# A trunk kernel with routed experts: gates applied at a place's last down product, plain turns of the small chunks, and VectorE in program order

## The chip, the cores and the metric

The kernel runs on one core of a Trainium2 chip. The core has TensorE for matrix products (PE in the profile), VectorE (DVE), ScalarE (ACT), GpSimd (POOL) and SyncE (SP), which here issues the loads of the weights; 16 DMA engines move the data. The metric is device time in microseconds (us) of one execution; less is better. All arithmetic is in float32. Where a product needs the precision of float32 at the pace of a rounded form, an operand is split in two rounded halves (a high and a low one) and the product is made of three.

## The reference, cut to what matters

The network has two layers. Each mixes 256 latent and 256 context tokens of width 1024 by three kinds of heads and then runs a feed-forward part. In the first layer that part is dense. In the second it is a choice of 2 among 8 experts per latent token, and only there does the change move work:

```python
def swiglu(h, wg, wu, wd):
    return (jax.nn.silu(h @ wg) * (h @ wu)) @ wd

def moe_ffn(h, w_r, wg, wu, wd):
    logits = (h @ w_r).astype(jnp.float32)
    top_v, top_i = lax.top_k(logits, TOP_K)
    gates = jax.nn.softmax(top_v, axis=-1)
    combine = jnp.sum(jax.nn.one_hot(top_i, N_EXPERTS, dtype=jnp.float32) * gates[..., None], axis=-2).astype(h.dtype)
    out = jnp.zeros_like(h)
    for e in range(N_EXPERTS):
        out = out + combine[..., e:e + 1] * swiglu(h, wg[e], wu[e], wd[e])
    return out
...
x = x + mod[5] * f        # f: what the experts gave; mod[5]: a factor per output column
```

Each expert has a gate and an up matrix of 1024 x 2816 and a down matrix of 2816 x 1024. All are read from HBM once: 264 pieces of 1 MB.

## The kernel before, in words

Tokens are sorted to the experts, and the experts by their load into eight places. Places 1, 0 and 2 are wide (128 slots for tokens), places 3, 4 and 5 have 64 slots, and places 7 and 6 have 32. A ninth set of 32 slots, the rest, holds what place 0 can't take. An expert's hidden width of 2816 is worked off in 11 chunks of 256 columns: two pieces of weights for gate and up, one for down.

A wide place takes each piece split: ScalarE writes the high half (`whi`, line 275), VectorE the low one (`wlo`, line 276), and TensorE multiplies with both into the bank `gu` (gate and up) and then the two banks `py` (down, `down`, line 1701). The small places are multiplied straight from the raw piece (`wraw`). Their chunk comes out with the slots in rows and must be turned: `narrow_mid` (line 1571) copies it to SBUF as `mid`, `turn` (line 1576) turns it on TensorE into the bank `mTx`, and `turned` (line 1584) makes silu times up from it (`silx`), which `down_small` (line 1735) multiplies into the bank `pys`. A 32-slot chunk lies in `mid` as two partial sums, one for each half of the contraction. Before, its turn is a product with a matrix `sel` of 64 columns, which adds the two on the way; a 64-slot chunk is turned by a plain transpose with the identity (`const`). The wide chunk's own product `sil` is transposed into a bank `mT` and split into `mh` and `ml`.

`rounds` (line 1523) interleaves them. First come rounds of place 7 alone; then the 11 rounds of place 1, the 11 of place 0 and the 11 of place 2, each round with one wide chunk and one or two small ones beside it (place 0's rounds have the rest as well); then two rounds of place 6 alone. Place 6 is the last.

When a place has had its last down product, a finish runs (`finishes` and `finish`, lines 1747 and 1754). VectorE multiplies the sum in PSUM with mod[5] into `y`, ScalarE and VectorE split `y` into `yh` and `yl`, TensorE multiplies both with the transposed one-hot `ohT` of the place (a bank `sc`), and VectorE adds the result, times the gate, to the output tile `acc`. A wide place does this in two halves of 512 columns, one after the other. `ohT` is made by `onehot` (line 1492): two compares on VectorE (`oh`), two transposes, a copy on ScalarE. Only one finish is under way at a time, whatever the place.

`sc`, `ohT`, `mT`, `mTx` and `xe` share two banks of PSUM in turn, so that each of them waits until the one before the last has been read.

Order. The program is emitted by a foreground (`experts`) and by background generators that it polls (`finish`, `onehot`, `gather`); a clock kept by estimates decides which step is emitted next and when a piece's split is due. For the experts' part `MSB` says which engines keep that sequence: in `"pa"` TensorE and ScalarE do, and VectorE's instructions are put in order by the scheduler of the tile framework. SyncE loads the weights through seven raw buffers.

Of the kernel before, what the change touches and what calls it, by code (L numbers as in the profile page):

```python
# [18 lines left out]
P = 128  # L19
D = 1024  # L20
KB = D // P
# [4 lines left out]
NE = 8  # L26
# [3 lines left out]
EPS = 1e-6  # L30
# [179 lines left out]
def until(cond):  # L210
    while not cond():
        yield 0.5
# [128 lines left out]
class Net:  # L341
# [1150 lines left out]
    def onehot(self, p):  # L1492

        nc = self.nc
        yield from until(lambda: len(self.ohT) < 2)
        self.ohT[p] = None
        oh = self.mp.tile([P, 2, P], F32, tag="oh1", name="oh1", bufs=1)
        n = self.slots(p)
        for t in range(2):
            nc.vector.tensor_scalar(oh[:, t, :].rearrange("p (a b) -> p a b", b=n), self.c("iota", 0, n).unsqueeze(1).to_broadcast([P, P // n, n]),  # L1500
                                    self.pos0[:, t, 0:1] if p == NE - 1 else self.pos[:, t, p:p + 1], None, op0=ALU.is_equal)
        yield 1.5
        pt = self.bank("ohT")
        for t in range(2):
            self.tp(pt[:, P * t:P * t + P], oh[:, t, :])
        ohT = self.mp.tile([P, 2, P], F32R, tag="ohT", name="ohT", bufs=2)
        nc.scalar.activation(ohT.rearrange("p a b -> p (a b)"), pt[:, :256], AF.Copy)
        yield 1.0
        self.ohT[p] = ohT

    SU = 4.0
    YB, YH = 1, 1
# [63 lines left out]
    def turn(self, pt, at, v, m):  # L1576
        for j in range(2):
            b = v[:, P * j:P * j + P]
            if m == 32:
                self.mm(pt[:, at + 64 * j:at + 64 * j + 64], b, self.sel, True, True)  # L1580
            else:
                self.tp(pt[:, at + P * j:at + P * j + P], b)

    def turned(self, pt, at, m):

        src = pt[:, at:at + 4 * m].rearrange("p (j g s) -> p j g s", j=2, g=2)
        s = self.mp.tile([P, 2, m], F32, tag=f"silx{m}", name="silx", bufs=5 if m == 32 else 4)
        self.act_fn(s, src[:, :, 0, :], AF.Silu)
        self.nc.vector.tensor_tensor(s, s, src[:, :, 1, :], op=ALU.mult)
        return s  # L1590

    def experts(self):
# [4 lines left out]
        nc, o = self.nc, self.o  # L1597
        self.xe, self.ohT, self.py = {}, {}, {}
        self.finishing = False
        self.ndone = 0  # L1600
        self.sel = self.mp.tile([P, 64], F32, name="sel", bufs=1)
        nc.vector.tensor_tensor(self.sel, self.c("ident", 0, 64), self.c("swap", 0, 64), op=ALU.add)
        o.spawn(self.gather(0), 2)
        pw, pn = None, []
        for w, ns in self.rounds() + [(None, [])]:
# [5 lines left out]
            if w:  # L1611
                p, c = w
                x = self.xe[p]
# [3 lines left out]
                for i in range(2):  # L1617
                    t = self.w.get(("gu", p, c, i))
# [34 lines left out]
            mids = []  # L1653
# [23 lines left out]
            if mids:  # L1677
                pt, at = self.bank("mTx"), 0
                for *_, m, v in mids:
                    self.turn(pt, at, v, m)  # L1680
                    at += 4 * m
            pw = None
            if w:
                pm = self.bank("mT")
                for j in range(2):
                    self.tp(pm[:, P * j:P * j + P], sil[:, P * j:P * j + P])
                mh = self.mp.tile([P, 256], F32R, tag="mh", name="mh", bufs=1)
                ml = self.mp.tile([P, 256], F32R, tag="ml", name="ml", bufs=1)
                self.split(mh, ml, pm[:, :256])
                pw = [*w, mh, ml, None]  # L1690
            at = 0
            for p, c, m, v in mids:
                mx = self.turned(pt, at, m)
                at += 4 * m
                if p == NE:
                    pw[4] = mx
                else:
                    pn.append((p, c, mx))
            yield

    def down(self, p, c, mh, ml):
# [12 lines left out]
        if z and p:  # L1714
            self.o.spawn(self.finishes(p), 1)
        return w

    def down_rest(self, w, c, mx):
# [13 lines left out]
        if c == NCH - 1:  # L1732
            self.o.spawn(self.finishes(0), 1)

    def down_small(self, p, c, mx):
# [8 lines left out]
        if c == NCH - 1:  # L1744
            self.o.spawn(self.finishes(p), 1)

    def finishes(self, p):
        yield from until(lambda: not self.finishing)
        self.finishing = True
        for q in (p, NE) if p == 0 else (p,):  # L1750
            yield from self.finish(q)
        self.finishing = False

    def finish(self, p):

        nc = self.nc
        m = self.slots(p)
        parts = P // m
        w = 512 if m > 32 else 256
        yield from until(lambda: self.ohT.get(p) is not None)  # L1760
        ohT = self.ohT[p]
        for n in range(2 if m == P else 1):
            yh, yl = (self.mp.tile([P, 512], F32R, tag=nm, name=nm, bufs=self.YH) for nm in ("yh", "yl"))
# [8 lines left out]
            yield 3.0  # L1772
            for g in (n,) if m == P else range(parts):
                cs = slice(w * g, w * g + w)
                rows = slice(m * g, m * g + m) if parts > 1 else slice(0, P)
                for t in range(2):
                    pz = self.bank("sc")
                    for i, v in enumerate((yh, yl)):
                        self.mm(pz[:, :w], ohT[rows, t, :], v[rows, :w], i == 0, i == 1)
                    nc.vector.scalar_tensor_tensor(self.acc[:, t, cs], pz[:, :w], self.gate[:, t, p:p + 1], self.acc[:, t, cs],  # L1780
                                                   op0=ALU.mult, op1=ALU.add)
                    if self.ndone == NE:
                        nc.sync.dma_start(self.out[P * t:P * t + P, cs], self.acc[:, t, cs])
                    yield 1.0
        del self.ohT[p]
        self.ndone += 1

# [80 lines left out]
    MSA, MSB = "", "pa"  # L1868
# [6 lines left out]
    def run(self):  # L1875
# [7 lines left out]
        with tc.tile_pool(name="keep", bufs=1) as keep, ExitStack() as self.pools, ExitStack() as self.kax, tc.tile_pool(name="sm", bufs=2) as self.sp, \  # L1883
# [3 lines left out]
            self.csil = keep.tile([P, KB, 38], F32, name="csil")  # L1887
            self.eps = keep.tile([P, 1], F32, name="eps")
            self.modT = [keep.tile([P, 48, 2], F32, name=f"modT{l}") for l in range(2)]
            self.wr = keep.tile([P, KB, NE], F32, name="wr")  # L1890
            self.acoef = keep.tile([P, 16], F32, name="acoef")
            self.nsink = keep.tile([P, 16], F32, name="nsink")
            nc.scalar.dma_start(self.csil, d["cT"])
            self.act_fn(self.csil, self.csil, AF.Silu)
            nc.scalar.dma_start(self.params, d["params"])
            nc.scalar.dma_start(self.const[:, :2 * P], d["consts"][:, :2 * P])
            nc.vector.memset(self.eps, EPS)
            self.act_fn(self.acoef, self.par("a_log"), AF.Exp)
            nc.vector.tensor_scalar(self.acoef, self.acoef, -1.0, None, op0=ALU.mult)
            nc.vector.tensor_scalar(self.nsink, self.par("sink"), -1.0, None, op0=ALU.mult)  # L1900
            self.nb, self.nc_banks = 4, 3
            self.w = Weights(self, self.plan(), self.nraw, self.nhi)
            with tc.tile_pool(name="psA", bufs=4, space=PSUM) as self.pp, tc.tile_pool(name="g", bufs=self.ng) as self.gp:
                self.ka = self.kax.enter_context(tc.tile_pool(name="keepA", bufs=1))
                self.gb = self.kax.enter_context(tc.tile_pool(name="act", bufs=2 * KB))
# [39 lines left out]
```

## Time and profile before

| what | us |
| --- | --- |
| three runs | 1587.26, 1581.52, 1585.33 |
| median | 1585.33 |
| the profiled execution | 1583.83 |
| its span, first to last instruction | 1582.1 |

The profile is of one execution on one core. The experts' part takes roughly its last third, from about 900 us on. The profile's page gives the busy time of each engine and the span in 40 slices; the trace answers questions on stretches (the windows) and on single instructions in order of time (the timeline). A timeline row has the start, the duration, the engine, the line, the operation, output and inputs, a count, and in brackets how long the engine had sat idle and which instruction released it. The mean granted clock of TensorE is 0.978 of full speed.

### The profile page before, as it was taken

The page shows a single profiled execution, that of the slowest core. Times are in us where ns is not written, and L with a number is a line of the kernel's source. Part 1 is how long each engine was busy: PE and PEld are TensorE (multiplying, and loading weights), DVE is VectorE, ACT ScalarE, POOL GpSimd, SP SyncE. Part 2 cuts the span into 40 slices and gives each one's busy share as a digit, 9 for nine tenths or more (in the row PEclk, how much of TensorE's full clock was granted, in tenths as well). Part 3 has the DMA queues.
Part 4 walks back from the last instruction along what each step waited for, and adds up shares of the span by engine and source line. Part 5 has one row for each costly group of instructions (what it writes and reads, how often), then busy time and mean ns, then how long its engine had stood idle before and what let it go on. Part 6 is the DMA issues. An engine that isn't in the chain of part 4 may idle for free. (4 is left out here: it accounts for less than half of the span.)

```text
span 1582.1 us, 23498 instructions
## 1 busy us (share of the span) xinstructions
PE 1500.2 (95%) x9302; PEld 1081.1 (68%) x9303; DVE 821.2 (52%) x1481; ACT 666.7 (42%) x1189; POOL 102.6 (6%) x135
## 2 busy tenths in 40 slices
PE   5999998899999999999999899999999999999997
PEld 1766675787887787878757776666566666656654
DVE  2687568543232333378774344544465444654545
ACT  3566644443222312266455354444343443433441
POOL 1200123210000000030300000000000000000000
PEclk9999999999999999999999899999999999999998
DMA  9422055333323323333164499999998999999994
GB/s 372 152 106 107 28 211 202 133 133 112 129 91 149 133 107 113 112 141 142 56 267 181 152 418 419 419 419 420 418 390 358 371 413 417 419 402 407 419 420 158
DMA packets 57715, 396.10 MB, mean 250 GB/s; under 512 B 6528, under 2 KB 8576, under 8 KB 10496
## 3 DMA queue, kind: packets, MB, share of 16 engines
q1 hardware_dynamic: 56016, 392.03, 62.2%
q10 hardware_dynamic: 1584, 2.52, 0.4%
q8 instruction: 75, 1.23, 0.3%
q14 instruction: 40, 0.33, 0.1%
HBM read 393.47 MB, written 1.05 MB: 249 GB/s over the span
## 5 line engine op out<-in xcount | busy, mean ns | idle before, releaser
L276 DVE TENSOR_TENSOR wlo<-wraw,whi 128x1024 fp32r<-128x1024 f32 (+2 forms) x318 | 377.0, 1222 | 161.2 <-ACT whi L275 155.9
L275 ACT ACTIVATE whi<-wraw 128x1024 fp32r<-128x1024 f32 (+2 forms) x318 | 320.0, 1047 | 148.5 <-PE fd L374 57.9
L374 PE MATMUL gu<-whi,xw 128*128 128x512 f32 x528 | 169.1, 401 | 4.2 <-ACT whi L275 4.2
L374 PE MATMUL gu<-wraw,xs 128*64 128x256 f32 (+1 forms) x1760 | 166.2, 386 | 0.5 <-ACT xs L1484 0.5
L374 PEld LDWEIGHTS gu<-wraw,xs 128*64 128x64 f32 (+1 forms) x1760 | 94.4, 127 | 64.3 <-issue 14.6
L374 PEld LDWEIGHTS gu<-whi,xw 128*128 128x128 f32 x528 | 96.9, 190 | 24.5 <-ACT whi L275 6.1
L374 PE MATMUL gu<-wlo,xw 128*128 128x512 f32 x264 | 104.9, 397 | 3.5 <-DVE wlo L276 3.5
L1162 DVE TENSOR_TENSOR fsil<-fsil,fu 128x512 f32<-128x512 f32 x22 | 15.1, 688 | 153.5 <-PE fu L374 118.2
L374 PE MATMUL pys<-wraw,silx 128*32 128x256 f32 (+1 forms) x616 | 87.6, 480 | 6.8 <-DVE y L1770 4.1
L425 ACT ACTIVATE fsil<-fg 128x512 f32<-128x512 f32 x22 | 13.1, 598 | 174.3 <-PE fg L374 174.3
L1573 ACT ACTIVATE mid<-gu 128x256 f32<-128x256 f32 x55 | 21.0, 382 | 137.1 <-PE gu L374 137.1
L374 PE MATMUL fg<-ahi,whi 128*128 128x512 f32 (+1 forms) x192 | 72.3, 377 | 0.0
L374 PE MATMUL fg<-alo,whi 128*128 128x512 f32 (+1 forms) x192 | 71.6, 373 | 0.2 <-POOL alo L523 0.2
L374 PE MATMUL fg<-ahi,wlo 128*128 128x512 f32 (+1 forms) x192 | 71.4, 372 | 0.0
L374 PE MATMUL fu<-alo,whi 128*128 128x512 f32 (+1 forms) x192 | 71.4, 372 | 0.0
L374 PE MATMUL fu<-ahi,wlo 128*128 128x512 f32 (+1 forms) x192 | 71.3, 372 | 0.0
L374 PE MATMUL fu<-ahi,whi 128*128 128x512 f32 (+1 forms) x192 | 71.3, 372 | 0.0
L374 PE MATMUL fd<-mhi,whi 128*128 128x512 f32 (+1 forms) x188 | 70.7, 376 | 0.0
L374 PE MATMUL fd<-mlo,whi 128*128 128x512 f32 (+1 forms) x188 | 70.6, 375 | 0.0
L374 PE MATMUL fd<-mhi,wlo 128*128 128x512 f32 (+1 forms) x188 | 70.6, 375 | 0.0
L374 PE MATMUL modp<-wraw,csil 128*32 128x512 f32 x384 | 56.7, 628 | 12.0 <-ACT csil L425 6.9
L374 PEld LDWEIGHTS gu<-wlo,xw 128*128 128x128 f32 x264 | 49.9, 189 | 18.3 <-DVE wlo L276 7.4
(342 smaller groups left out, 2831.8 us busy)
## 6 DMA issues: line engine op xcount, KB each, us to landing
wraw<-in_moe_dram SPq DMA_DIRECT2D x264, 1024.0 KB, 12.6
wraw<-in_wmod_dram SPq DMA_DIRECT2D x48, 1024.0 KB, 6.4
wraw<-in_fgu_dram SPq DMA_DIRECT2D x22, 1024.0 KB, 4.8
wraw<-in_win_dram SPq DMA_DIRECT2D x16, 1024.0 KB, 4.9
wraw<-in_wout_dram SPq DMA_DIRECT2D x8, 1024.0 KB, 6.2
wraw<-in_fdn_dram SPq DMA_DIRECT2D x8, 1024.0 KB, 6.2
wraw<-in_fdn_dram SPq DMA_DIRECT2D x4, 768.0 KB, 4.9
wraw<-in_wgd_dram SPq DMA_DIRECT2D x2, 1056.0 KB, 4.9
```

Of the source, the lines that this page charges most:

```text
L275: nc.scalar.activation(hi[:, cs], t[:, cs], AF.Copy)
L276: nc.vector.tensor_tensor(lo[:, cs], t[:, cs], hi[:, cs].bitcast(F32), op=ALU.subtract)
L374: self.nc.tensor.matmul(out, l, r, start=start, stop=stop)
L425: self.last_act = self.nc.scalar.activation(out, in_, func, **kw)
L1162: self.nc.vector.tensor_tensor(s, s, pu, op=ALU.mult)
L1573: self.nc.scalar.activation(v, ps[:, :256], AF.Copy)
```

## The change

Five things. (1) The multiplication by mod[5] and the split into halves (`halves`) are emitted at once when a place's last down product is emitted, not when the finish's turn comes; for wide places both halves of the columns, in a buffer `fin`. Wide and narrow finishes no longer wait for each other, only for one of their own kind. The scatter products `sc` follow later. (2) A 32-slot chunk is turned by two plain transposes of 128 columns; ScalarE then copies one partial sum out of the bank to a tile `sum`, and VectorE adds the other, before silu. Two turns share one bank, the wide chunk's among them. (3) VectorE too follows the program's sequence in the experts' part (`MSB = "pad"`). (4) Three `ohT` buffers instead of two. (5) Some small tiles of the first part move to a pool that is freed before the experts' part. The instructions of GpSimd and SyncE stand in the same order before and after, and so does everything ahead of the experts' part on the other engines.

```diff
     def onehot(self, p):
-        yield from until(lambda: len(self.ohT) < 2)
+        yield from until(lambda: len(self.ohT) < 3)
...
-    def turn(self, pt, at, v, m):
+    def turn(self, pt, at, v):
         for j in range(2):
-            b = v[:, P * j:P * j + P]
-            if m == 32:
-                self.mm(pt[:, at + 64 * j:at + 64 * j + 64], b, self.sel, True, True)
-            else:
-                self.tp(pt[:, at + P * j:at + P * j + P], b)
+            self.tp(pt[:, at + P * j:at + P * j + P], v[:, P * j:P * j + P])
 
     def turned(self, pt, at, m):
-        src = pt[:, at:at + 4 * m].rearrange("p (j g s) -> p j g s", j=2, g=2)
+        src = pt[:, at:at + 256]
+        if m == 32:
+            v = src.rearrange("p (j r c) -> p j r c", j=2, r=2)
+            src = self.mp.tile([P, 2, 64], F32, tag="sum32", name="sum32", bufs=2)
+            self.nc.scalar.activation(src, v[:, :, 0, :], AF.Copy)
+            self.nc.vector.tensor_tensor(src, src, v[:, :, 1, :], op=ALU.add)
+            src = src.rearrange("p j (g s) -> p j g s", g=2)
...
-            if mids:
-                pt, at = self.bank("mTx"), 0
-                for *_, m, v in mids:
-                    self.turn(pt, at, v, m)
-                    at += 4 * m
+            jobs = [[x, x[3]] for x in mids] + ([[None, sil]] if w else [])
+            for i, x in enumerate(jobs):
+                if i % 2 == 0:
+                    pt = self.bank("mT" if i + 1 == len(jobs) else "mTx")
+                self.turn(pt, 256 * (i % 2), x[1])
+                x[1] = pt
...
         if z and p:
-            self.o.spawn(self.finishes(p), 1)
+            self.finished(p)
...
+    def halves(self, p):
+        nc, m = self.nc, self.slots(p)
         parts = P // m
         w = 512 if m > 32 else 256
-            yh, yl = (self.mp.tile([P, 512], F32R, tag=nm, name=nm, bufs=self.YH) for nm in ("yh", "yl"))
+        if m == P:
+            f = self.mp.tile([P, 2, KB, P], F32R, tag="xw", name="fin", bufs=2).rearrange("p a k s -> p (a k s)")
+            ys = [(f[:, 1024 * n:1024 * n + 512], f[:, 1024 * n + 512:1024 * n + 1024]) for n in range(2)]
+        else:
+            ys = [tuple(self.mp.tile([P, 512], F32R, tag=nm, name=nm, bufs=1) for nm in ("yh", "yl"))]
+        for n, (yh, yl) in enumerate(ys):
             y = self.mp.tile([P, 512], F32, tag="xsum", name="y", bufs=self.YB)
...
+    def finished(self, p):
+        self.o.wait(lambda: not self.finishing[self.wide(p)])
+        self.o.spawn(self.finishes(p), 1)
+        self.o.poll()
+
+    def finish(self, p, ys):
...
+        yield max(3.0, self.w.splits - self.o.clk + 3.0)
+        yield from until(lambda: self.ohT.get(p) is not None)
+        ohT = self.ohT[p]
+        if p == self.last:
+            yield from until(lambda: self.ndone == NE)
...
-    MSA, MSB = "", "pa"
+    MSA, MSB = "", "pad"
```

Where the rounds of place 1 end and those of place 0 begin, VectorE had this order before. `y<-py` is the gating of place 1, `acc` the additions of its scatter, `wlo` the splits for place 0, `ml` the split of place 0's first chunk, and `y<-pys` the gating of a 64-slot place that ends in the same round.

```order
L1766 TENSOR_TENSOR y<-py,mod5row 128x512
L438 TENSOR_TENSOR yl<-y,yh 128x512
L1766 TENSOR_TENSOR y<-py,mod5row 128x512
L1780 SCALAR_TENSOR_TENSOR acc<-sc,gate,acc 128x512 x2
L276 TENSOR_TENSOR wlo<-wraw,whi 128x1024 x4
L438 TENSOR_TENSOR yl<-y,yh 128x512
L438 TENSOR_TENSOR ml<-mT,mh 128x256
L1589 TENSOR_TENSOR silx<-silx,mTx 128x64
L1770 TENSOR_TENSOR y<-pys,mod5row 64x512
L1589 TENSOR_TENSOR silx<-silx,mTx 128x128
```

In the changed kernel VectorE has this at the same place; `fin` is the low half of the split of `y`.

```order
L438 TENSOR_TENSOR fin<-y,fin 128x512
L276 TENSOR_TENSOR wlo<-wraw,whi 128x1024
L1500 TENSOR_SCALAR oh_9283<-const,pose 128x128 x2
L276 TENSOR_TENSOR wlo<-wraw,whi 128x1024
L1806 SCALAR_TENSOR_TENSOR acc<-sc,gate,acc 128x512
L276 TENSOR_TENSOR wlo<-wraw,whi 128x1024 x2
L1806 SCALAR_TENSOR_TENSOR acc<-sc,gate,acc 128x512 x2
L1767 TENSOR_TENSOR y<-pys,mod5row 64x512 x2
L438 TENSOR_TENSOR yl<-y,yh 128x512
L438 TENSOR_TENSOR ml<-mT,mh 128x256
L1587 TENSOR_TENSOR sum_9359<-sum_9359,mTx 128x128
```

The one-hot compares, three of place 1's additions and the gating of the 64-slot place now stand ahead of `ml`.

On TensorE the same place reads so in the changed kernel, from the last half of the 64-slot chunk to place 0's next wide chunk.

```order
L374 MATMUL sc<-fin,ohT 128x512 x2
L379 MATMUL ohT<-const,oh_9283 128x128 x2
L374 MATMUL gu<-wraw,xs_7662 64x256 x8
L374 MATMUL sc<-fin,ohT 128x512 x2
L374 MATMUL pys<-wraw,silx 64x512 x4
L374 MATMUL sc<-fin,ohT 128x512 x2
L379 MATMUL mTx<-const,mid 128x128 x4
L379 MATMUL mT<-const,sil 128x128 x2
L374 MATMUL sc<-fin,ohT 128x512 x2
L374 MATMUL gu<-whi,xw 128x512 x2
```

Before, two of the four scatter products stood ahead of `mTx`, the other two stood among place 0's products behind it, and the transposes of the one-hot came a round later.

At the end of the program VectorE had this order before, from the gating of place 2 (`y<-py`) to that of the last place (`y<-pys` with 32x256); `silx` with 128x64 is place 6's.

```order
L1780 SCALAR_TENSOR_TENSOR acc<-sc,gate,acc 128x512
L1589 TENSOR_TENSOR silx<-silx,mTx 128x64
L1780 SCALAR_TENSOR_TENSOR acc<-sc,gate,acc 128x512
L438 TENSOR_TENSOR yl<-y,yh 128x512
L1770 TENSOR_TENSOR y<-pys,mod5row 64x512 x2
L1589 TENSOR_TENSOR silx<-silx,mTx 128x64
L1780 SCALAR_TENSOR_TENSOR acc<-sc,gate,acc 128x512 x2
L438 TENSOR_TENSOR yl<-y,yh 128x512
```

In the changed kernel the end of VectorE's order is this.

```order
L1806 SCALAR_TENSOR_TENSOR acc<-sc,gate,acc 128x512
L1767 TENSOR_TENSOR y<-pys,mod5row 64x512 x2
L438 TENSOR_TENSOR yl<-y,yh 128x512
L1587 TENSOR_TENSOR sum_12686<-sum_12686,mT 128x128
L1593 TENSOR_TENSOR silx<-silx,sum_12686 128x64
L1806 SCALAR_TENSOR_TENSOR acc<-sc,gate,acc 128x512 x5
L1500 TENSOR_SCALAR oh_12739<-const,pos 128x128 x2
L1587 TENSOR_TENSOR sum_12745<-sum_12745,mT 128x128
L1593 TENSOR_TENSOR silx<-silx,sum_12745 128x64
L1806 SCALAR_TENSOR_TENSOR acc<-sc,gate,acc 128x512 x2
L1767 TENSOR_TENSOR y<-pys,mod5row 32x256 x4
```

Six additions and the last one-hot now stand ahead of the last chunk's `silx`, where three stood before.

## Rows read from the trace of the kernel before

**Rows 1.** The page: busy time of each engine, its share, its instructions.

```profile
PE 1500.2 (95%) x9302; PEld 1081.1 (68%) x9303; DVE 821.2 (52%) x1481; ACT 666.7 (42%) x1189; POOL 102.6 (6%) x135
```

**Rows 2.** Windows: length, busy us of PE, PEld, DVE, ACT, POOL; clock, DMA, GB/s.

```profile
1000.00:1100.00 100.00, 96.62 (x660) 63.69 (x653) 45.98 (x57) 45.72 (x76) 0.00 (x0) 1.00 1.01 419
1100.00:1200.00 100.00, 95.04 (x667) 60.65 (x669) 54.48 (x82) 38.33 (x64) 0.00 (x0) 0.98 0.96 395
1200.00:1300.00 100.00, 99.62 (x826) 67.73 (x818) 46.37 (x63) 45.41 (x77) 0.00 (x0) 1.00 0.95 385
...
1380.00:1390.00 10.00, 5.88 (x32) 2.13 (x26) 5.86 (x7) 1.75 (x3) 0.00 (x0) 0.77 1.01 419
1400.00:1410.00 10.00, 10.00 (x85) 5.69 (x85) 5.04 (x7) 2.87 (x5) 0.00 (x0) 1.00 0.93 350
1440.00:1450.00 10.00, 10.00 (x64) 6.68 (x64) 4.89 (x7) 4.19 (x7) 0.00 (x0) 1.00 0.98 367
```

**Rows 3.** Timeline of PE where place 1 ends and place 0 begins.

```profile
1142.84 0.66 PE L374 MATMUL mTx<-sel,mid 128*128 128x64 f32 x4
1143.34 0.39 PE L379 MATMUL mTx<-const,mid 128*128 128x128 f32 x2
1143.56 0.38 PE L379 MATMUL mT<-const,sil 128*128 128x128 f32 x2
1143.70 0.71 PE L374 MATMUL gu<-whi,xw 128*128 128x512 f32 x2
...
1147.36 0.50 PE L374 MATMUL sc<-yh,ohT 128*128 128x512 f32 x1 [0.66 <-DVE ml L438]
```

**Rows 4.** Timeline of DVE at the same place.

```profile
1133.04 0.69 DVE L1766 TENSOR_TENSOR y<-py,mod5row 128x512 f32<-128x512 f32 x1 [0.59 <-PE py L374]
...
1141.75 4.62 DVE L276 TENSOR_TENSOR wlo<-wraw,whi 128x1024 fp32r<-128x1024 f32 x4
```

**Rows 5.** Groups by form on DVE and ACT, 1100 to 1582 us: busy, mean ns.

```profile
L276 DVE TENSOR_TENSOR wlo<-wraw,whi 128x1024 fp32r<-128x1024 f32 x138 | 162.8, 1220 | 71.5 <-ACT whi L275 70.9
L1780 DVE SCALAR_TENSOR_TENSOR acc<-sc,gate,acc 128x512 f32<-128x512 f32 x24 | 17.8, 750 | 28.0 <-PE sc L374 27.7
L438 DVE TENSOR_TENSOR ml<-mT,mh 128x256 fp32r<-128x256 f32 x24 | 10.2, 423 | 39.5 <-ACT mh L437 39.0
L1589 DVE TENSOR_TENSOR silx<-silx,mTx 128x128 f32<-128x128 f32 x24 | 6.8, 283 | 5.5 <-ACT silx L425 5.5
L438 DVE TENSOR_TENSOR yl<-y,yh 128x512 fp32r<-128x512 f32 x9 | 6.2, 685 | 1.0 <-ACT yh L437 1.0
L1770 DVE TENSOR_TENSOR y<-pys,mod5row 64x512 f32<-64x512 f32 x6 | 4.1, 687 | 0.1
L425 ACT ACTIVATE silx<-mTx 128x128 f32<-128x128 f32 x24 | 6.6, 276 | 9.8 <-DVE silx L1589 9.8
L437 ACT ACTIVATE yh<-y 128x512 fp32r<-128x512 f32 x9 | 5.6, 625 | 9.1 <-DVE y L1766 5.4 <-PE sc L374 3.7
```

**Rows 6.** Timeline of PE around place 0's first wide products.

```profile
1120.42 0.73 PE L374 MATMUL gu<-whi,xw 128*128 128x512 f32 x2 [2.37 <-ACT whi L275]
...
1122.75 1.05 PE L374 MATMUL gu<-whi,xw 128*128 128x512 f32 x2
...
1126.58 0.62 PE L374 MATMUL gu<-whi,xw 128*128 128x512 f32 x2
```

**Rows 7.** Timeline of PE where place 0 ends and place 2 begins.

```profile
1387.12 3.68 PE L374 MATMUL pys<-wraw,silx 128*64 128x512 f32 x8 [4.12 <-DVE y L1770]
```

**Rows 8.** Timeline of PE at the end.

```profile
1561.05 1.07 PE L374 MATMUL pys<-wraw,silx 128*32 128x256 f32 x16 [0.67 <-DVE silx L1589]
...
1570.88 0.57 PE L374 MATMUL sc<-yh,ohT 32*128 32x256 f32 x1 [2.68 <-ACT yh L437]
```

**Rows 9.** Timeline of DVE at the end.

```profile
1557.96 0.75 DVE L1780 SCALAR_TENSOR_TENSOR acc<-sc,gate,acc 128x512 f32<-128x512 f32 x1 [1.18 <-PE sc L374]
...
1576.06 0.91 DVE L1780 SCALAR_TENSOR_TENSOR acc<-sc,gate,acc 128x256 f32<-128x256 f32 x2 [0.46 <-PE sc L374]
```

More of the change, by code (lines that the diff above doesn't have):

```diff
@@ L1511 @@
     SU = 4.0
-    YB, YH = 1, 1
+    YB = 1
     NRAW, MKRAW = 4, 5
@@ L1598, in experts @@
         self.xe, self.ohT, self.py = {}, {}, {}
-        self.finishing = False
+        self.finishing = [False, False]
         self.ndone = 0
-        self.sel = self.mp.tile([P, 64], F32, name="sel", bufs=1)
-        nc.vector.tensor_tensor(self.sel, self.c("ident", 0, 64), self.c("swap", 0, 64), op=ALU.add)
+        self.last = self.steps()[-1][1]
         o.spawn(self.gather(0), 2)
@@ L1732, in down_rest @@
         if c == NCH - 1:
-            self.o.spawn(self.finishes(0), 1)
+            self.finished(0)
     def down_small(self, p, c, mx):
@@ L1744, in down_small @@
         if c == NCH - 1:
[L1745 to L1757, printed above, removed]
+            self.finished(p)
+    def halves(self, p):
+        nc, m = self.nc, self.slots(p)
         parts = P // m
         w = 512 if m > 32 else 256
-        yield from until(lambda: self.ohT.get(p) is not None)
-        ohT = self.ohT[p]
-        for n in range(2 if m == P else 1):
-            yh, yl = (self.mp.tile([P, 512], F32R, tag=nm, name=nm, bufs=self.YH) for nm in ("yh", "yl"))
+        if m == P:
+            f = self.mp.tile([P, 2, KB, P], F32R, tag="xw", name="fin", bufs=2).rearrange("p a k s -> p (a k s)")
+            ys = [(f[:, 1024 * n:1024 * n + 512], f[:, 1024 * n + 512:1024 * n + 1024]) for n in range(2)]
+        else:
+            ys = [tuple(self.mp.tile([P, 512], F32R, tag=nm, name=nm, bufs=1) for nm in ("yh", "yl"))]
+        for n, (yh, yl) in enumerate(ys):
             y = self.mp.tile([P, 512], F32, tag="xsum", name="y", bufs=self.YB)
@@ L1771, in finish @@
             self.split(yh[:, :w], yl[:, :w], y[:, :w])
[L1772 to L1784, printed above, removed]
+        return ys
@@ new lines, in finishes, with begin @@
+    def finishes(self, p):
+        yield from self.finish(p, self.begin(p))
+        if p == 0:
+            yield from until(lambda: not self.finishing[False])
+            yield from self.finish(NE, self.begin(NE))
+    def begin(self, p):
+        self.finishing[self.wide(p)] = True
+        return self.halves(p)
+    def finished(self, p):
[3 more added lines that the diff above has]
+    def finish(self, p, ys):
+        nc = self.nc
+        m = self.slots(p)
+        parts = P // m
+        w = 512 if m > 32 else 256
+        wide = m == P
+        yield max(3.0, self.w.splits - self.o.clk + 3.0)
[3 more added lines that the diff above has]
+            yield from until(lambda: self.ndone == NE)
+        for g in range(D // w):
+            cs = slice(w * g, w * g + w)
+            rows = slice(0, P) if wide else slice(m * g, m * g + m)
+            for t in range(2):
+                pz = self.bank("sc")
+                for i, v in enumerate(ys[g if wide else 0]):
+                    self.mm(pz[:, :w], ohT[rows, t, :], v[rows, :w], i == 0, i == 1)
+                nc.vector.scalar_tensor_tensor(self.acc[:, t, cs], pz[:, :w], self.gate[:, t, p:p + 1], self.acc[:, t, cs],
+                                               op0=ALU.mult, op1=ALU.add)
+                if p == self.last:
+                    nc.sync.dma_start(self.out[P * t:P * t + P, cs], self.acc[:, t, cs])
+                yield 1.0
@@ L1785, in finish @@
         del self.ohT[p]
         self.ndone += 1
+        self.finishing[wide] = False
     def overflow(self):
@@ L1886, in run @@
             self.params = keep.tile([P, NPARAM], F32, name="params")
-            self.csil = keep.tile([P, KB, 38], F32, name="csil")
             self.eps = keep.tile([P, 1], F32, name="eps")
-            self.modT = [keep.tile([P, 48, 2], F32, name=f"modT{l}") for l in range(2)]
+            self.modT = [None, keep.tile([P, 48, 2], F32, name="modT1")]
             self.wr = keep.tile([P, KB, NE], F32, name="wr")
[L1891 to L1900, printed above, removed]
             self.nb, self.nc_banks = 4, 3
```

30 lines of the change are left out of this document (21 added, 9 removed).

## The prediction, made before the changed kernel ran

> **What bounds the kernel now.** I read the page first, then windows over the experts' part, then the timeline at the places where the change moves instructions. TensorE is busy for 95% of the span, VectorE for 52% and ScalarE for 42% [rows 1]. In the experts' part TensorE shares the bound with the loads, and the windows show which of the two holds where [rows 2]. While place 1 runs (1000 to 1100 us) the loads move 419 GB/s, the most any long window shows, and TensorE has 3.4 us idle in 100: the loads bound it. While place 0 runs, with the rest beside it, TensorE has 0.4 us idle in 1200 to 1300 and the loads fall to 385 GB/s: TensorE bounds it. The two windows from 1100 to 1300 lose (419 - 395) / 419 x 100 = 5.7 and (419 - 385) / 419 x 100 = 8.1, so 13.8 us of transfer that never comes back: any us added to or taken from TensorE there, up to that size, moves the end by the same. From 1400 on the loads are full but for two windows at 350 and 367 GB/s, together 1.65 + 1.24 = 2.9 us; a gain of TensorE there can bring no more than that. After the loads end, what is left is one chain at the end of the program. So the change counts in three places: from place 1's end through place 0, from place 0 to place 2, and at the end. In place 1's own rounds an idle TensorE has slack, and what changes there I cost at nothing; the cover is the loads, and were they not the bound there, a turn's waits, some 0.4 us a round, would cost 4 us.
>
> **Place 1 to place 0.** VectorE before had the gating of place 1 at 1133.04, two additions, and by the order four splits (4.62 us) ahead of `ml` [rows 4]; place 0's second wide chunk began on TensorE at 1143.70 [rows 3]. In the changed order I follow VectorE from 1133.04 with the durations of [rows 5]: two gatings of 0.69, each followed by ScalarE's half (0.63) and VectorE's (0.69), to 1137.1; a split of 1.22 to 1138.3; the two one-hot compares (0.28 each, taken like the `silx` of 0.28) to 1138.9; a split to 1140.1; an addition of 0.75 to 1140.9; two splits to 1143.3; two additions to 1144.8; two gatings of the 64-slot place to 1146.2; ScalarE's half to 1146.8; `yl` to 1147.5; then `ml` 0.42, with hand-overs about 1148.5 to 1149. The fourth `sc` on TensorE takes the bank of `mT`, so it waits for `ml`, and the wide chunk stands right behind that `sc`. With its pair of about 0.6 us the wide chunk starts at 1149.8 instead of 1143.70, 6.1 later. Of this, two scatter pairs (2 x 0.6) and the one-hot's transposes (0.44) are work that came later before, and the stall of 0.66 behind `ml` goes [rows 3]. What is left is 6.1 - 1.65 - 0.66 = 3.8 us of new idle time on TensorE: 1.2 before the one-hot's transposes, the rest before the fourth `sc`. Bounds: 1 us if the hand-overs overlap better than I drew them, 6 if one more split is late.
>
> Such a wait has a second price. After a stall of 2.37 us at 1120.42 a pair of products took 1.05 us instead of 0.62 for a while, and at 1126.58 it was back [rows 6]; the granted clock was then at the lower of its two levels (1.2 of 2.4 GHz). About 3 us at half pace cost 1.5; the same after the new stall, 0 to 2. ScalarE's first high half behind `mh` comes 0.3 later, as `sum` is ahead of it. When place 7 finishes in the same way, its `mT` waits for an addition behind two splits: 1 us (0 to 2.5).
>
> **Turns.** Four passes with `sel` take 0.50 us from start to start (1142.84 to 1143.34), two transposes 0.22 [rows 3]. A 32-slot chunk so gains 0.25 to 0.28 on TensorE. Of the 33 such chunks 12 to 13 lie where TensorE is the bound: 12.5 x 0.25 = -3.1 (0 to -3.5). In exchange ScalarE gets a copy of about 0.28 and VectorE an addition of about 0.29 for each, 33 x 0.29 = 9.6 us each over the experts' part; both have half their time free, and the splits stand around them. I cost them at nothing; without that cover, in place 0's rounds, they would cost about as much as the turns gain.
>
> A bank with two turns has readers on two engines. The trace before has this already: ScalarE waited 9.8 us in all for VectorE's `silx` before its own, 24 times, 0.41 us each [rows 5]. The Trainium skill says, in "PSUM — Partial Sum Buffer", section "PSUM bank collisions raise a hardware error", that two engines must not touch the same bank at once, even at other columns, and that semaphores should guard by bank; the trace agrees, since those two `silx` read different columns. By that rule alone the sum would carry another 11 rounds x 0.4 = 4.4 us if none of it were hidden, and by the row none, as ScalarE's waits fell in its free time. I go by the row.
>
> Sum of this place: 3.8 + 1.5 + 0.3 + 1.0 - 3.1 = +3.5, paid in full since TensorE bounds the stage.
>
> **Place 0 to place 2.** The gating of a 64-slot place came late on VectorE before, behind a split, and TensorE stood for 4.12 us and then ran eight products in 3.68 us [rows 7], the window at a clock of 0.77 [rows 2]. In the new order the gating follows the last down product of its place, so these 4.1 us and about 2.2 us of low clock go. In their place come small waits: the turn for a bank whose addition stands behind two splits, the halves of the first pieces behind `yh` and `mh`, 2.5 us by the same walk. TensorE gains 3.8, but the loads ran at 419 GB/s through the stall [rows 2] and lose only the 2.9 us above afterwards. I take half: -1.5 (0 to -2.9).
>
> **The end.** Before, place 2's second addition ended at 1558.7 [rows 9], place 6's last down product began at 1561.05 after 0.67 us of waiting [rows 8], and the last scatter waited 2.68 us for ScalarE's `yh` at 1570.88 [rows 8]. Now the gating of the 64-slot place (1.39), its `yl` (0.69) and the turn's addition and `silx` (0.5) stand between the first and the second addition, which ends at 1561.0. The next scatter waits for it, and the last down product behind it, with six additions, the one-hot and a turn ahead, ends at about 1567.3 instead of 1562.1. Then the scatter, the one-hot's transposes and copy, two additions to 1570.5, four gatings (4 x 0.43) and `yh` to 1572.7, against 1570.88 for the scatter behind it before. The last eight scatter pairs are the same, so the last addition ends 1.9 us later than 1576.97. With some low clock in the new gaps I take +2.5 (0 to +5).
>
> **Sum.** 3.5 - 1.5 + 2.5 = +4.5 on the profiled execution's 1583.83 (span 1582.1, 1.7 around it): 1588.3. The median of the runs is 1.5 above that execution, which is inside the spread of the three runs; I forecast 1588.0.
>
> **Rivals.** What this kernel's runs can tell from no change is about 0.5%, 7.9 us: faster means under 1577.4, slower over 1593.3.
>
> A, the gains pass and the waits don't come. The walk over VectorE is mine, and the planner that wrote this order had its own estimate of when each input is there. If the idle time at 1143 is 1 us without a drop of the clock, the turns give their 3.5, the second place its 2.9 and the end 0, the sum is 1 + 0.3 - 3.5 - 2.9 = -5.1: 1579. For it: VectorE is half idle [rows 1], and the only long wait of TensorE for VectorE's gating, 4.12 us, is removed [rows 7]. Against it: at the end and at place 0's start the rows put the new order's inputs behind work of known length. If further drops of the clock vanish it goes below 1577.4.
>
> B, the fixed sequence on VectorE turns each finish into a stall. One mechanism: an addition `acc` that waits for its `sc` now holds the splits behind it, and a split that waits for `whi` holds the addition that would free a bank. There are nine finishes; if six of them hold TensorE for 1.2 us (a split's length [rows 5]) and then cost 1 us of low clock, that is 13 us, less 3.1 and 1.5, plus the end: 1593 to 1597, say 1595. It decides once the walk's waits occur at four or more finishes in the part that TensorE bounds. For it: additions had 28.0 us of waiting for `sc` ahead of them [rows 5], which before other work could fill. Against it: in place 1's rounds the loads hide this.
>
> C, nothing of it reaches the end, since the waits only change places: the loads set the pace of all but the last chain, place 0's rounds get back from the turns what its start loses, and the last chain comes out as before: 1584 to 1585. Against it: the 13.8 us of lost transfer say that place 0's rounds are not the loads' [rows 2].
>
> **How the numbers follow.** Forecast (1583 to 1593) 0.50, A 0.22, B 0.20, C 0.08. A is split: 0.12 of it below 1577.4, the rest within. B: 0.16 above 1593.3; the forecast's upper terms (6 for 3.8, 5 for 2.5) add 0.04. So faster 0.12, same 0.68, slower 0.20. The lows together give 1 + 0 + 0.3 + 0 - 3.5 - 2.9 + 0 = -5.1, and the highs 6 + 2 + 0.3 + 2.5 + 0 + 0 + 5 = +15.8. The range leaves out the tenth at either side: 1577 to 1597; the likeliest case's own is 1583 to 1593.
>
> **What would show it.** In the profile after: TensorE idle for about 3 us before a `sc<-fin` with `ml` as the releaser, just before place 0's second wide chunk (right: the 3.8); no wait of `pys` for `y` of 4 us where place 2 begins; two transposes of 0.22 us in the place of `sel`; loads still short of 419 GB/s in place 0's rounds; the last down product ending 4 to 5 us later in relation to the end of the loads. Wrong would be: waits on `acc` or `ml` at most finishes (B), or a start of place 2 that is early by more than 5 us (A).

## The result: slower by about 1%, and the profile after

Four runs of the changed kernel took 1599.46, 1605.89, 1598.7 and 1598.38 us, median 1599.08, against 1586.2 for the kernel before (four runs). The ratio is 1.0105, 95% interval 1.0083 to 1.0128. The forecast of 1588.0 was 11 us short, and the range, 1577 to 1597, ended 2 us below the median. The profiled execution took 1599.46 us (span 1597.6), 15.6 more than that of before.

Where these lie is read from the timelines of TensorE by marks that both kernels have. A round's mark is the start of the transposes of its wide chunk's `sil`; rounds 1 to 11 are place 1's, 12 to 22 place 0's, 23 to 33 place 2's.

| mark | before | changed | later by |
| --- | --- | --- | --- |
| last transposes ahead of the experts' part | 887.67 | 894.02 | 6.35 |
| round 1 | 939.65 | 949.39 | 9.74 |
| round 11 | 1117.66 | 1128.03 | 10.37 |
| round 12 | 1143.56 | 1156.42 | 12.86 |
| round 13 | 1168.46 | 1183.69 | 15.23 |
| round 15 | 1211.77 | 1228.42 | 16.65 |
| round 22 | 1350.90 | 1365.36 | 14.46 |
| round 26 | 1430.81 | 1441.46 | 10.65 |
| round 33 | 1546.49 | 1557.66 | 11.17 |
| last scatter product | 1576.03 | 1591.33 | 15.30 |

The windows of the changed kernel that answer to [rows 2], and one where the loads paused (length, busy us by engine, clock, DMA share, GB/s):

```profile
940.00:950.00 10.00, 9.52 (x72) 6.47 (x71) 6.58 (x7) 5.88 (x9) 0.00 (x0) 1.00 0.83 309
...
1000.00:1100.00 100.00, 95.22 (x609) 63.77 (x609) 49.12 (x66) 48.02 (x83) 0.00 (x0) 1.00 1.01 419
1100.00:1200.00 100.00, 92.18 (x670) 57.39 (x670) 52.44 (x77) 38.50 (x67) 0.00 (x0) 0.97 0.92 377
1200.00:1300.00 100.00, 97.90 (x780) 65.44 (x780) 48.57 (x75) 44.29 (x82) 0.00 (x0) 0.98 0.92 372
```

The first of them, where the loads paused, answers to this one of the kernel before, ten us earlier, in which they ran at full rate:

```profile
930.00:940.00 10.00, 9.52 (x72) 6.44 (x71) 6.37 (x6) 5.03 (x7) 0.00 (x0) 1.00 1.01 418
```

TensorE idles more and the loads move less from 1100 to 1300 us, as they would where TensorE is the bound. Where place 1 ends (timeline of PE; it answers to [rows 3]):

```profile
1149.98 0.53 PE L379 MATMUL ohT<-const,oh 128*128 128x128 f32 x2 [0.80 <-DVE oh L1500]
...
1156.42 0.44 PE L379 MATMUL mT<-const,sil 128*128 128x128 f32 x2 [0.41 <-DVE acc L1806]
1159.56 1.00 PE L374 MATMUL sc<-fin,ohT 128*128 128x512 f32 x2 [2.70 <-DVE ml L438]
1160.36 1.05 PE L374 MATMUL gu<-whi,xw 128*128 128x512 f32 x2
...
1163.77 0.62 PE L374 MATMUL gu<-whi,xw 128*128 128x512 f32 x2
```

and VectorE there (answers to [rows 4]):

```profile
1151.90 2.36 DVE L276 TENSOR_TENSOR wlo<-wraw,whi 128x1024 fp32r<-128x1024 f32 x2
...
1156.28 1.38 DVE L1767 TENSOR_TENSOR y<-pys,mod5row 64x512 f32<-64x512 f32 x2
1158.35 0.69 DVE L438 TENSOR_TENSOR yl<-y,yh 128x512 fp32r<-128x512 f32 x1 [0.69 <-ACT yh L437]
1159.08 0.42 DVE L438 TENSOR_TENSOR ml<-mT,mh 128x256 fp32r<-128x256 f32 x1
```

The fourth scatter waits 2.70 us for `ml`, the place's wide chunk stands behind it, and its first pairs run at half pace (1.05 us; by 1163.77 a pair takes 0.62 again). At round 14's mark, where place 7 finishes, `mT` waits 1.26 us for an addition:

```profile
1203.91 0.44 PE L379 MATMUL mT<-const,sil 128*128 128x128 f32 x2 [1.26 <-DVE acc L1806]
```

The 4.12 us of `pys` waiting for `y` where place 2 began [rows 7] are gone. The end (PE; answers to [rows 8]):

```profile
1578.67 1.07 PE L374 MATMUL pys<-wraw,silx 128*32 128x256 f32 x16 [1.53 <-DVE silx L1593]
...
1586.18 0.57 PE L374 MATMUL sc<-yh,ohT 32*128 32x256 f32 x1 [2.98 <-ACT yh L437]
```

Two stretches stand in no term of the forecast. The first is ahead of the experts' part, where both kernels issue the same instructions. The second is between it and round 1. There place 3 to 5's tokens are gathered (`xe`), and TensorE waits for their one-hot. Changed kernel, PE:

```profile
927.31 1.57 PE L374 MATMUL pys<-wraw,silx 128*32 128x256 f32 x16 [2.81 <-DVE silx L1593]
931.30 7.04 PE L374 MATMUL xe<-oh,hr 128*128 128x192 f32 x32 [2.42 <-DVE oh L1466]
```

Kernel before, PE:

```profile
920.20 1.07 PE L374 MATMUL pys<-wraw,silx 128*32 128x256 f32 x16 [2.00 <-DVE silx L1589]
921.21 7.15 PE L374 MATMUL xe<-oh,hr 128*128 128x192 f32 x32
```

Changed kernel, VectorE:

```profile
927.98 2.36 DVE L276 TENSOR_TENSOR wlo<-wraw,whi 128x1024 fp32r<-128x1024 f32 x2 [0.72 <-ACT whi L275]
930.25 1.06 DVE L1466 TENSOR_SCALAR oh<-const,pos 128x64 f32<-128x64 f32 x6
```

Kernel before, VectorE:

```profile
915.69 0.74 DVE L1466 TENSOR_SCALAR oh<-const,pos 128x64 f32<-128x64 f32 x4 [5.80 <-PE xe L374]
...
916.95 0.41 DVE L1466 TENSOR_SCALAR oh<-const,pos 128x64 f32<-128x64 f32 x2
...
920.38 3.50 DVE L276 TENSOR_TENSOR wlo<-wraw,whi 128x1024 fp32r<-128x1024 f32 x3 [0.23 <-ACT whi L275]
```

In program order the compares stand behind two splits, which wait for ScalarE. Before, the scheduler had put them ahead of the splits, and the gather followed at 921.21 without a wait. The wait for the one-hot stands in all three traces in which VectorE follows the program (2.42 us here, 2.91 and 2.92 in two of the kernels below) and in none of the others.

### The profile page after: what moved, and what is told of

Its sections match the earlier page's. It is cut to its first block, busy times and chain, and to the rows that moved or that the text cites. A ratio compares the mean times of both kernels' runs of the same rounds, so it can differ in the third digit from the quotient of the medians.

```text
span 1597.6 us, 23437 instructions
## 1 busy us (share of the span) xinstructions
PE 1505.6 (94%) x9236; PEld 1074.6 (67%) x9237; DVE 830.4 (52%) x1513; ACT 675.1 (42%) x1222; POOL 103.1 (6%) x135
## 3 DMA queue, kind: packets, MB, share of 16 engines
HBM read 393.47 MB, written 1.05 MB: 247 GB/s over the span
```

## Experiments

All were run beside the kernel before on their chip; ratios are to it, with 95% intervals.

**The moved tiles alone.** The changed kernel's edit of the pools, on the kernel before.

```diff
-            self.csil = keep.tile([P, KB, 38], F32, name="csil")
+                self.csil = self.ka.tile([P, KB, 38], F32, name="csil")
...   # modT0, acoef and nsink alike
```

> The kernel before with only its four small tiles moved to the freed pool, so that the pools of the weights and of the first part's tiles begin 1728 bytes lower and nothing else differs. Theory (place in SBUF): the changed kernel lost 6.3 us ahead of the experts' part because the first layer's products read from other addresses; then this kernel loses the same, its product of gate and up in the dense part goes from 0.2267 to about 0.2333 us from start to start, its experts' part starts 6 us late, and the median is 5 to 7 us above the kernel before, about 1592. Rival (that stretch differs between any two executions): the products keep 0.2267 us, and the median stays within 2 us of before.

Measured: 1588.48 against 1582.41, ratio 1.0042 (1.0026 to 1.0057), and the marks 5.58 us late at round 1 and 5.31 at round 33. So the move alone costs it, and nothing more is lost behind it. In the dense part, the first layer's feed-forward, TensorE never idles, and a window of 200 us holds fewer products than before. The kernel before:

```profile
400.00:600.00 200.00, 200.00 (x902) 162.77 (x901) 68.85 (x93) 47.32 (x58) 0.00 (x0) 1.00 0.32 114
```

The moved tiles alone:

```profile
400.00:600.00 200.00, 200.00 (x887) 160.45 (x886) 66.58 (x92) 46.62 (x58) 0.00 (x0) 1.00 0.32 116
```

From start to start the products of gate and up (`fg`, `fu`) take 0.2272 us before and 0.2334 here, those of down (`fd`) 0.2267 and 0.2269, as means over the products with 512 moving columns (the expectations' 0.2267 is what most single ones take). By the code the moving operand of down lies in a pool that moved together with the weights, that of gate and up in one that stayed.

**The changed kernel with 448 bytes of padding.**

```diff
+            self.gap = keep.tile([P, 112], F32, name="gap")
```

> The changed kernel with an unused tile of 448 bytes in the first pool, so that the weights' tiles lie 1280 bytes below where they lay before instead of 1728 (the same place within 256 bytes as before, another within 512). Theory (place within a line of up to 256 bytes): the dense part is as fast as before, 6 us come back, about 1593. Rival one (the place within a longer line, or the distance to the other operand decides): still about 1599, or another value between. Rival two (not the place at all): 1599 with the same 0.2333 us.

Measured: 1601.34, ratio 1.0115 (1.0093 to 1.0136), with `fg` and `fu` at 0.2333. The theory of the weights' own place falls. But the padding had moved the activations too, since their pool lies above: the distance between the two had stayed as in the changed kernel. That gave the theory of the next test.

**The moved tiles in a pool opened last.** Weights and dense activations then both lie 1728 bytes lower (8 x 38 x 4 + 48 x 2 x 4 + 2 x 16 x 4) than in the kernel before.

```diff
-                self.csil = self.ka.tile([P, KB, 38], F32, name="csil")
+                self.kt = self.kax.enter_context(tc.tile_pool(name="keepT", bufs=1))   # after act and xp
+                self.csil = self.kt.tile([P, KB, 38], F32, name="csil")
```

> The kernel before with the four moved tiles in a pool that is opened last in the first part: the weights' tiles begin 1728 bytes lower as in the kernel with only the move, and so do the activations of the dense part, which that kernel left where they were. Theory (the place of the weights relative to the moving operand decides; the down products, where both had moved together, kept their pace): gate and up of the dense part are back at 0.2267 us from start to start, and the median is within 2 us of the kernel before. Rival (the weights' own place, or the move itself): 6 us above before, as with only the move.

Measured: ratio 0.9999 (0.9983 to 1.0015), and the window is as before:

```profile
400.00:600.00 200.00, 200.00 (x901) 162.78 (x900) 68.88 (x93) 47.32 (x58) 0.00 (x0) 1.00 0.32 114
```

So the distance between the two operands decides. Two more kernels, with one execution each, change it by an unused tile ahead of the activations.

```diff
+                self.gap = self.ka.tile([P, 16], F32, name="gap")     # 64 bytes; 64 columns for 256
```

> The kernel before with the moved tiles in the pool opened last, and an unused tile of 64 bytes ahead of the activations of the dense part, so that they lie 64 bytes further from the weights. Theory (pace by the distance within 256 bytes): gate and up of the dense part go at a pace other than 0.2267 us; 0.2333 if any distance but zero is slow. Rival (only a distance near 1728 or 192 is slow): 0.2267, and the dense part ends with the kernel before.

> The same with 256 bytes. Theory (within 256 bytes): 0.2267 us and no loss in the dense part. Rival (within a longer line, or the absolute distance): slower by 5 us there.

With 64 bytes:

```profile
400.00:600.00 200.00, 200.00 (x896) 161.97 (x896) 68.88 (x93) 47.37 (x58) 0.00 (x0) 1.00 0.31 113
```

With 256 bytes:

```profile
400.00:600.00 200.00, 200.00 (x901) 162.75 (x900) 68.88 (x93) 47.33 (x58) 0.00 (x0) 1.00 0.32 114
```

`fg` and `fu` take 0.2290 us at 64 bytes and 0.2272 at 256. The two executions took 1582.69 and 1583.51 us; a single execution can't tell 2 us in the total, so the reading is of the pace alone. From the first product with 512 moving columns to the last of down it is 351.9 us at a distance of 0 or 256 bytes more, 353.7 at 64 and 357.9 at 1728 (6 x 256 + 192). The 192 products of gate and up with 256 moving columns, ahead of these, went the other way, from 0.120 us to 0.114 at 1728. So from the first product of gate to the last of down the moved tiles cost 4.9 us (375.5 to 380.4).

**The changed kernel with VectorE ordered by the scheduler.**

```diff
-    MSA, MSB = "", "pad"
+    MSA, MSB = "", "pa"
```

> The changed kernel with VectorE again ordered by the scheduler and not by the program's sequence. Theory (the fixed sequence on VectorE costs the experts' part its time): the wait of 2.4 us for the one-hot at the first gather goes (3.4 us between the start and the first wide chunk), the wait of 2.7 us for ml and that of 0.8 us for the one-hot at place 0's start shrink, and the end is 2 us shorter: 1599 - 3 - 3 - 2, about 1590 to 1592. Rival (the new order on TensorE and the gating at the last down product make these waits, whatever VectorE's order): 1597 to 1600.

Measured: 1591.63, ratio 1.006 (1.0045 to 1.0076); the padded changed kernel took 1601.34 on the same chip. The gather's wait is gone (the marks are 4.37 us late ahead of the experts' part and 4.16 at round 1, so nothing is lost between them), and the stretch from round 33 to the last scatter, 33.7 us in the changed kernel, is 29.9 (before: 29.5). But place 0's start got worse, not better, and rounds 12 and 13 take 58.3 us (before 50.8, changed 55.7):

```profile
1156.17 1.22 PE L374 MATMUL sc<-fin,ohT 128*128 128x512 f32 x2 [5.51 <-DVE ml L438]
```

So the total followed the theory, and that part of it the rival: this wait comes with the new order on TensorE, whoever orders VectorE.

**The plain turns alone** (with the moved tiles as in the first experiment).

```diff
-                self.mm(pt[:, at + 64 * j:at + 64 * j + 64], b, self.sel, True, True)
+            self.tp(pt[:, at + P * j:at + P * j + P], v[:, P * j:P * j + P])
...   # and the copy, the addition and the shared banks
```

> The kernel before with the moved tiles and the plain turns alone. Theory (each 32-slot chunk gains 0.25 us where TensorE is the bound): 2 to 3 us below the kernel with only the moved tiles, shown between the second and the ninth round of place 0. Rival (the added copy, addition and shared bank on ScalarE and VectorE take back what TensorE gains): the same as the kernel with only the moved tiles, or up to 4 us above.

Measured: 1589.19, ratio 1.0046 (1.0028 to 1.0063), the same as with the moved tiles alone: the rival's number. By the marks the turns do gain: 2.7 us on that kernel at round 22 and 3.5 at round 23. Then it goes, and round 33 is 0.8 later. In place 2's rounds the stall of [rows 7] is still there, and ScalarE, with the added copy ahead of its splits, is a little later (PE):

```profile
1390.98 3.56 PE L374 MATMUL pys<-wraw,silx 128*64 128x512 f32 x8 [4.12 <-DVE y L1772]
...
1468.04 0.73 PE L374 MATMUL gu<-whi,xw 128*128 128x512 f32 x2 [1.18 <-ACT whi L275]
1469.30 0.76 PE L374 MATMUL gu<-wlo,xw 128*128 128x512 f32 x1 [0.53 <-DVE wlo L276]
1469.86 1.05 PE L374 MATMUL gu<-whi,xw 128*128 128x512 f32 x2
```

The same wait was 0.94 us with the moved tiles alone, and no low clock followed it; here a pair behind it takes 1.05 us. The moved tiles alone:

```profile
1470.21 0.73 PE L374 MATMUL gu<-whi,xw 128*128 128x512 f32 x2 [0.94 <-ACT whi L275]
...
1471.81 0.62 PE L374 MATMUL gu<-whi,xw 128*128 128x512 f32 x2
```

**The changed kernel with the scatter products of wide places spread** (tiles in the pool opened last).

```diff
-                yield 1.0
+                yield 4.0 if wide else 1.0
```

> The changed kernel with the moved tiles in the pool opened last, and with 4 us instead of 1 on the planner's clock between the scatter products of a wide finish, so that two of the four come behind place 0's wide chunk. VectorE still follows the program. Theory (at place 0's start TensorE waited because the fourth scatter took the bank that ml still read, and ml stood behind the gating and additions): the wait of 2.7 us and its low clock go; the two rounds there, which took 2.5 and 2.4 us more than before, take at most 1 more each; with 5.5 from the first part the median is 1590 to 1592. Rival (what stands ahead of ml on VectorE is late by itself, and the wait moves to the next product that needs ml): the two rounds stay 4 to 5 us longer, 1593 to 1595.

Measured: 1581.04, ratio 0.9994 (0.9979 to 1.0009), 10 us under what the theory gave. At place 0's start the wide chunk follows the turn at once (PE):

```profile
1149.03 0.44 PE L379 MATMUL mT<-const,sil 128*128 128x128 f32 x2 [0.41 <-DVE acc L1806]
1149.22 0.71 PE L374 MATMUL gu<-whi,xw 128*128 128x512 f32 x2
```

Rounds 12 and 13 take 51.0 us (before 50.8, changed 55.7), so this part holds. The theory had not seen that the same scatters cost elsewhere: round 15 takes 22.92 instead of 24.51, round 29 16.67 instead of 19.67, and the end from round 33 on 30.5 instead of 33.7. The rest is the start of the experts' part, 8.3 us earlier than in the changed kernel (6.6 at round 1), 2.7 more than the distance explains: among the kernels with a fast distance it came from 3.4 us earlier to 2.0 later than in the kernel before, though they issue the same instructions up to there. Why it differs is open, and a single trace's start is no finer measure than that.

**The gating at the last down product alone** (tiles in the pool opened last, turns with the matrix, scheduler's order on VectorE).

```diff
-            self.o.spawn(self.finishes(p), 1)
+            self.finished(p)
...   # and halves, begin and finish as in the change
```

> The kernel before with the gating at the last down product alone (moved tiles in the pool opened last, turns with the added matrix, VectorE ordered by the scheduler). Theory (the new place of the scatter products costs 7 us at place 0's start, as in the changed kernel with the scheduler's order, the removed wait of 4.1 us brings back 2 to 3, and the end does nothing): 3 to 5 us above before, 1586 to 1588. Rival (with the shorter turn on ScalarE and VectorE the wait at place 0's start shrinks to 2 us): the same as before or up to 3 us faster.

Measured: 1581.72, ratio 1.0 (0.9982 to 1.0017): the rival's number with the theory's mechanism. (In the traced execution, of 1578.88 us, the experts' part began 3.4 us earlier than in the kernel before and was 1.6 us shorter.) The wait is there in full (PE):

```profile
1146.40 1.22 PE L374 MATMUL sc<-fin,ohT 128*128 128x512 f32 x2 [5.28 <-DVE ml L438]
```

and costs 6.0 us between rounds 11 and 13, of which 1.8 came back in round 14. At place 2's start the stall of [rows 7] is gone; round 23 lost 2.4 to a wait of `mT` for an addition, rounds 24 to 26 gave 5.4, so 2.9 is left of it by then, as much as the prediction's bound for this stage; but rounds 27 to 33 gave another 1.5, so more came back behind the stall than that bound allowed.

**The spread with VectorE ordered by the scheduler** (the rest as in the spread kernel).

```diff
-    MSA, MSB = "", "pad"
+    MSA, MSB = "", "pa"
```

> As the kernel with the spread scatter products, but VectorE ordered by the scheduler. Theory: the gather's 3.4 us and the end's 4 us are the fixed sequence's and go with it, the wait of 5.5 us that this order had at place 0's start goes with the spread, and the first part is as before: 1579 to 1583, level with the kernel before or just under. Rival (the waits at place 0's start only move): 1586 to 1588.

Measured: 1580.9, ratio 0.9981 (0.9967 to 0.9995): the theory. Its interval overlaps with that of the program's sequence, so once the scatters are spread the sequence on VectorE costs nothing in the total that these runs can tell. By the two traces it trades: the scheduler's order is 4.7 us shorter from the start of the experts' part to round 1 and 3.1 from round 33 to the last scatter, but its rounds 12 and 13 take 54.0 us against 51.0, and rounds 23 and 24 take 42.6 against 38.4.

**The gating alone, spread.** Both edits together, without plain turns.

```diff
+            self.finished(p)
...
+                yield 4.0 if wide else 1.0
```

> The kernel with the gating at the last down product alone (matrix turns, scheduler's order on VectorE, tiles moved to the pool opened last), with the wide finish's scatter products spread by 4 us on the planner's clock. Theory (its 5.3 us of waiting for ml at place 0's start and the low clock after it go, and TensorE bounds that stage, so the gain passes): round 12, 30.5 us without the spread, takes 25 to 27, and the median is 3 to 5 us below the kernel without the spread, 1577 to 1579. Rival (place 2's rounds, which the loads bound, take it back as they took the turns' gain): 1580 to 1582.

Measured: 1576.39, ratio 0.9959 (0.9943 to 0.9975), the best version: faster than the kernel before by 0.4%, where the changed kernel is slower by 1%. In the traces the experts' part itself is 6.9 us shorter than before. The stretch from mark 12 to mark 13 (the expectation's round 12) takes 27.9 us, a little above the theory's range. It still has waits of that kind (PE):

```profile
1146.16 0.50 PE L374 MATMUL sc<-yh,ohT 64*128 64x512 f32 x1 [1.91 <-DVE ml L438]
...
1372.15 0.73 PE L374 MATMUL sc<-fin,ohT 128*128 128x512 f32 x2 [1.62 <-DVE ml L438]
```

**The narrow places spread as well** (on the kernel two above, so with plain turns).

```diff
-                yield 4.0 if wide else 1.0
+                yield 1.0 if p == self.last else 4.0 if wide else 2.5
```

> The kernel with all of the change but the scheduler's order on VectorE, the moved tiles in the pool opened last and the wide scatter products spread by 4, and with 2.5 between the narrow places' scatter products too (not the last place's). Theory (its waits of 1.9 and 1.2 us of a narrow place's scatter for ml, each with low clock behind it, go): 3 us below the kernel without it, 1577 to 1579. Rival (bound by the loads in place 2's rounds): 1580 to 1582.

Measured: 1587.49, ratio 1.0033 (1.0016 to 1.0049). Both theories fall. A scatter of a 32-slot place now stands half a wide chunk behind a turn of four chunks, where none stood before, and still waits for the bank that VectorE's addition reads; another waits for `ml` (PE):

```profile
1222.45 0.35 PE L374 MATMUL sc<-yh,ohT 32*128 32x256 f32 x1 [2.20 <-DVE sum L1587]
...
1417.04 0.38 PE L374 MATMUL sc<-yh,ohT 32*128 32x256 f32 x1 [1.64 <-DVE ml L438]
```

The round of the first takes 22.66 us instead of 17.91. By these rows it counts where a scatter falls behind a turn, not how far apart the scatters are.

## Why the prediction was wrong, point by point

- **Place 1 to place 0** (3.8 + 1.5 + 0.3 + 1.0 = 6.6): right. Rounds 12 to 15 lost 16.65 - 10.37 = 6.3 us. The new waits were 0.80 for the one-hot, 0.41 for the addition and 2.70 for `ml`, 3.9 against the 3.8 of the walk; the pairs behind took 1.05 us, and place 7's finish cost a wait of 1.26 for the 1.0.
- **Turns** (-3.1): right in place 0's rounds. The turns alone gain 3.1 from round 11 to 22, 0.6 of it in rounds 12 to 15; here it is -2.2 from round 15 to 22. Wrong that it would be paid in full: alone, place 2's rounds took it all.
- **Place 0 to place 2** (-1.5, 0 to -2.9): -3.3 from round 22 to 33, twice the term and a little beyond the bound.
- **The end** (+2.5, 0 to +5): 15.30 - 11.17 = +4.1. Inside the bounds, but 1.6 more than the term. The order of the walk was right: the last down product waited 1.53 us and the last place's first scatter 2.98.
- These four give 6.3 - 2.2 - 3.3 + 4.1 = +4.9, against the forecast's +4.5. That the sum is so close is luck: by these stretches the terms are off by -0.3, +0.9, -1.8 and +1.6, and the last two cancel.
- **What failed first**: "So the change counts in three places" leaves no term at all for the fifth edit, the moved tiles. It took equal instructions for equal time ahead of the experts' part. There the changed kernel lost 6.4 us. The move alone cost 5.6 there (1.0042 in the total), and with the distance undone nothing (0.9999); 4.9 of it is seen in the pace of the dense part's products, and the rest lies within what the start differs by between traces.
- **What failed second**: "In place 1's own rounds an idle TensorE has slack, and what changes there I cost at nothing". Ahead of round 1 the changed kernel lost 3.4 us, and 0.6 more by round 11; with VectorE ordered by the scheduler the 3.4 are gone, so they are the fixed sequence's. The loads did not cover it: they fell to 309 GB/s at 940 us, where they had moved 418 before. SyncE waited up to 11.4 us there for a `wlo` to free a raw buffer (8.3 before). By this the loads hid a stall of TensorE only as far as buffers were free to load into, and as they bound the rounds that follow, the end got all of it.
- Together: 6.4 + 3.4 + 0.6 + 4.9 = 15.3 us, the last mark's delay.
- Rival B came nearer in time (1595) but not in place: it wanted waits at four or more finishes in the part that TensorE bounds, and there were two, at place 1's finish (2.70) and place 7's (1.26), both of which the sum already had.

## What to carry to other kernels

Walk the engine whose order changes through the durations of the old trace: where that was done, the waits came where the walk put them, and at place 0's start with the size it gave. Then ask for a term for every edit that has none, a move of tiles to another pool included: compare the addresses of the operands of the busiest products, not only the order of the instructions. And in this kernel a product that takes a bank behind a turn waits for the slowest reader of that turn; put it where that reader is done by the durations, not just later.

## What the runs showed of the hardware

The pace of a float32 product in rounded form with 128 columns of weights and 512 moving ones hung on the distance between the weights' and the moving operand's addresses in SBUF. At 0 and 256 bytes beyond the old distance it took 0.2272 us from start to start, at 64 bytes 0.2290, at 1728 bytes 0.2334, all at a granted clock of 1.00. The place of the weights alone does not decide: it is the same at 256 bytes, at 64 and in one of the layouts with the old distance. Products with 256 moving columns went the other way, 0.120 us at the old distance and 0.114 at 1728. That 0 and 256 are alike would fit a repeat every 256 bytes, but other distances were not tried.
